# A two-layer encoder trunk on one core: an earlier pool for the FFN up stage, one addition for v, and down tiles that alternate

## The chip, the cores and the metric

The kernel runs on one core of one Trainium2 chip. The metric is the device time of one execution in microseconds (us). Three runs of a kernel give its median.

## What is computed

512 positions of 1024 features go through two layers in float32. Each layer is a token mixer and a gated convolutional FFN, both behind an RMS norm and added to x. Layer 0's mixer joins four trailing-mean pools with a short gated convolution; layer 1's is gated linear attention. The FFN, which the change is mostly about:

```python
def conv_ffn(h, w_up, conv_w, conv_b, w_down):
    u, v = jnp.split(h @ w_up, 2, axis=-1)          # 1024 -> 2 x 2816
    u = causal_dwconv(u, conv_w, conv_b)            # 3 taps along the positions
    return (jax.nn.gelu(u, approximate=False) * v) @ w_down

def reference(x, ...):
    for l in range(DEPTH):                          # 2
        hn = rmsnorm(x, mix_norm[l])
        if l % 2 == 0: y = concat(pool_mixer(...), sb * causal_dwconv(sc * sx, ...)) @ ab_w_out
        else:          y = gla_mixer(hn @ gla_w_in, ...) @ gla_w_out
        x = x + y
        x = x + conv_ffn(rmsnorm(x, ffn_norm[l]), ...)
    return rmsnorm(x, final_norm)
```

## The kernel before

**Data and precision.** Features lie on the 128 partitions, the 512 positions along the free dimension. A float32 factor is split in two parts, hi (rounded by ScalarE, ACT) and lo (the rest, by VectorE, DVE), and a product is three passes of TensorE (PE) matmuls: hi·hi, hi·lo, lo·hi. `split` (L154) does this, with ACT at L155 and DVE at L156.

**Order.** One program is written out; the Tile framework keeps each engine's instructions about in the order of the calls and sets semaphores where a tile is written, read or its buffer reused. Each engine (PE, DVE, ACT, GpSimd or POOL, and SP, which issues the loads) then works through its own list in order. An instruction that waits holds up all behind it on its engine.

**Stages, in the profile's time.** Projections for layer 0's mixers (0 to 100 us), their output projection `abo` (to 144), the up stage of layer 0 (to 380), the down stage (to 500), attention (to 671), its output projection `go` (to 715), the up stage of layer 1 (to 947), the down stage and the final norm. `norm_rows` sums squares with PE, computes the reciprocal root on DVE (L267 to L275, the reciprocal at L271), forms `diag` (L285) and has PE broadcast it (`bc`, L296), which ACT copies to `rs`. `mix_out` also calls `mix_tokens`, which forms the sums and differences of x that the up stage needs (`th`, `tl`).

**Up stage.** 22 tiles of 128 columns for u and for v. The first and last are plain: 48 matmuls of 128x512. The other 20 ("S") use `seven`: the 2x2 block product (rows of w by halves, positions by halves) with seven half-size products p1 to p7 in place of eight, each of 12 matmuls of 128x256. Their weights are:

- a1, the raw left half (SP's load L447, 512 KB, one buffer serves the left halves in turn), split; read by p1 (first half) and p2 (second half)
- s31, a sum of two quarters: SP loads one quarter twice (L439), a GpSimd load adds two more to it (L443, an accumulating DMA); three buffers in the pool "up"; split for p5 and p7
- s2 = −s31 − left (DVE L469), in the free part of the right half's buffer; split into `sh`, `sl` for p6
- a2, the raw right half (SP's load L451, 256 KB) beside left − s2 (DVE L471), split; for p4 and p3

The split parts of a1, s31 and a2 go round four buffers (pool `wsp`). The products accumulate in three PSUM banks: x (p1, p6, p7, p4, with copies k1, k2, k3 taken by ACT in between), y (p2), z (p5, p3). Then

```python
u[hi_t] = -z - k3            # L533, after p7
u[lo_t] = -x                 # ACT, after p4;  u *= rs  L539
v[lo_t] = y + k1             # L520, after p2
v[hi_t] = z + k2             # L544, after p3
```

and u goes through the convolution (ACT L348, DVE L349 and L352) and Gelu (ACT L403); L545 multiplies with v. The steps of all tiles are sorted by hand-given times: tile j starts at `base`, PERIOD later than the one before, the products stand at base + LAYOUT[p], the loads and splits at the offsets in the code.

**Pools.** "side" (y_h of layer 0's mixers, attention's `vtok`, the last four m tiles) and "up" (s31, sh, sl) are opened in turn in one stretch of memory: `open_stage` closes the one and opens the other, so that the first tiles of "up" wait for the last reader of "side". At the start "side" is open; `ffn_up` opens "up", and "side" opens again at the last up tile.

**Down stage.** Eight output tiles; each takes 22 m tiles in blocks of 8, 7 and 7 with one load a block. `split_m` makes the hi and lo parts of m during the last plain tile.

## Time and profile before

| | |
|---|---|
| median of 3 runs | 1082.75 us (1082.29, 1082.75, 1085.55) |
| profiled execution, own time | 1081.99 us |
| its span, first to last instruction | 1080.3 us |
| mean granted TensorE clock | 0.989 |
| PE busy | 1047.6 us, 97% |
| DVE busy | 741.1 us, 69% |
| ACT busy | 543.4 us, 50% |
| GpSimd busy | 52.7 us, 5% |
| HBM read | 132.77 MB, 125 GB/s over the span |
| left and plain up loads of 512 KB, issue to landing | 4.0 us (median of 48) |
| s31 loads; accumulating loads | 4.7 us; 7.4 us (medians of 40) |

Durations in the profile are of one instruction. A row of the timeline gives start, duration, engine, line and operation, `out<-in` by the program's names, and in brackets the idle time of the engine before it with what ended it. Matmuls overlap, so their spacing, not their duration, is what counts. A row of the stretches gives the length, then the busy time of each engine with its count of instructions. In the profile the s31 tiles are called `s`, the copies `k`, the banks `stx`, `sty`, `stz`.

### The profile page before, as it was taken

The page shows a single profiled execution, that of the slowest core. Times are in us where ns is not written, and L with a number is a line of the kernel's source. Part 1 is how long each engine was busy: PE and PEld are TensorE (multiplying, and loading weights), DVE is VectorE, ACT ScalarE, POOL GpSimd, SP SyncE. Part 2 cuts the span into 40 slices and gives each one's busy share as a digit, 9 for nine tenths or more (in the row PEclk, how much of TensorE's full clock was granted, in tenths as well). Part 3 has the DMA queues.
Part 4 walks back from the last instruction along what each step waited for, and adds up shares of the span by engine and source line. Part 5 has one row for each costly group of instructions (what it writes and reads, how often), then busy time and mean ns, then how long its engine had stood idle before and what let it go on. Part 6 is the DMA issues. An engine that isn't in the chain of part 4 may idle for free.

```text
span 1080.3 us, 16455 instructions
## 1 busy us (share of the span) xinstructions
PE 1047.6 (97%) x6586; PEld 937.4 (87%) x6586; DVE 741.1 (69%) x1116; ACT 543.4 (50%) x825; POOL 52.7 (5%) x79
## 2 busy tenths in 40 slices
PE   9999978999999999999999999999999999999996
PEld 7788868999999988889988888879999999988886
DVE  6885758889888874335465565687888888873333
ACT  6342646656656662224773354565556656662221
POOL 0000010110110000000000001001010110000000
PEclk9999998999999999999999999999999999999998
DMA  6421276777765433323332117236777775433312
GB/s 221 144 78 59 79 178 171 186 190 174 186 167 136 130 90 108 97 86 106 94 104 93 42 43 172 63 114 155 168 183 177 184 180 128 130 89 109 96 47 78
DMA packets 53645, 135.94 MB, mean 126 GB/s; under 512 B 4704, under 2 KB 7136, under 8 KB 53568
## 3 DMA queue, kind: packets, MB, share of 16 engines
q1 hardware_dynamic: 41456, 112.74, 34.6%
q0 software_dynamic: 10880, 20.97, 11.9%
q10 hardware_dynamic: 1232, 1.17, 0.3%
q8 instruction: 51, 0.84, 0.3%
q14 instruction: 26, 0.21, 0.1%
HBM read 132.77 MB, written 2.10 MB: 125 GB/s over the span
## 4 chain that ended last, share of the span: by engine, by line
PE 65%; DVE 16%; DMA 11%; issue 6%; ACT 2%; DVEq 0%; SPq 0%; ACTq 0%
PE dn L239 22%; DMA raw<-in_w_up 9%; PE stx L502 7%; PE r L239 4%; PE abo L239 4%; PE go L239 4%; DVE lo L156 3%; PE q L239 2%; PE k L239 2%; PE px L239 2%; PE pb L239 2%; PE stz L502 2%; DVE raw L469 2%; DVE cacc L352 2%; DVE cacc L545 2%
## 5 line engine op out<-in xcount | busy, mean ns | idle before, releaser
L156 DVE TENSOR_TENSOR lo<-raw,hi 128x1024 fp32r<-128x1024 f32 (+2 forms) x191 | 227.7, 1192 | 90.8 <-PE dn L239 50.5
L155 ACT ACTIVATE hi<-raw 128x1024 fp32r<-128x1024 f32 (+2 forms) x191 | 197.3, 1034 | 182.4 <-PE dn L239 101.4
L348 ACT ACTIVATE cacc<-u,colt 128x512 f32<-128x512 f32 x48 | 39.2, 816 | 101.5 <-DVE u L539 91.8
L239 PE MATMUL dn<-mh,hi 128*128 128x512 f32 (+1 forms) x374 | 89.2, 377 | 0.0
L239 PE MATMUL dn<-mh,lo 128*128 128x512 f32 (+1 forms) x374 | 88.7, 377 | 0.0
L239 PE MATMUL dn<-ml,hi 128*128 128x512 f32 (+1 forms) x374 | 88.6, 376 | 0.0
L443 POOL DMA_DIRECT2D s<-in_w_up x40 | 48.2, 1205 | 696.1 <-DVE lo L156 219.3
L239 PEld LDWEIGHTS dn<-mh,hi 128*128 128x128 f32 x374 | 67.5, 188 | 13.4 <-ACT mh L155 0.5
L239 PEld LDWEIGHTS dn<-ml,hi 128*128 128x128 f32 x374 | 67.5, 188 | 12.9
L239 PEld LDWEIGHTS dn<-mh,lo 128*128 128x128 f32 x374 | 67.5, 188 | 12.8
L502 PE MATMUL stx<-th,hi 128*128 128x256 f32 x320 | 55.0, 294 | 8.0 <-ACT k L511 7.1
L349 DVE SCALAR_TENSOR_TENSOR cacc<-u,colt,cacc 128x511 f32<-128x511 f32 x48 | 36.0, 751 | 35.4 <-ACT cacc L348 35.4
L502 PEld LDWEIGHTS stx<-th,hi 128*128 128x128 f32 x320 | 42.8, 188 | 16.0 <-ACT k L511 15.1
L254 ACT ACTIVATE xh<-xall,colt 128x512 fp32r<-128x512 f32 x32 | 22.9, 721 | 59.7 <-DVE xall L334 58.8
L502 PE MATMUL stx<-tl,hi 128*128 128x256 f32 x320 | 49.7, 278 | 0.0
L502 PE MATMUL stx<-th,lo 128*128 128x256 f32 x320 | 49.7, 278 | 0.0
L156 DVE TENSOR_TENSOR lo<-s,hi 128x1024 fp32r<-128x1024 f32 x40 | 48.7, 1217 | 0.6 <-ACT hi L155 0.6
L155 ACT ACTIVATE hi<-s 128x1024 fp32r<-128x1024 f32 x40 | 41.9, 1048 | 9.9 <-DMA s<-in_w_up 9.3
L469 DVE SCALAR_TENSOR_TENSOR raw<-s,raw 128x512 f32<-128x512 f32 x40 | 27.6, 691 | 27.5 <-DMA raw<-in_w_up 17.8
L502 PEld LDWEIGHTS stx<-tl,hi 128*128 128x128 f32 x320 | 42.7, 188 | 0.0
L502 PEld LDWEIGHTS stx<-th,lo 128*128 128x128 f32 x320 | 42.6, 188 | 0.0
L511 ACT ACTIVATE k<-stx 128x256 f32<-128x256 f32 x120 | 40.6, 366 | 2.5 <-PE stx L502 2.4
(289 smaller groups left out, 2305.0 us busy)
## 6 DMA issues: line engine op xcount, KB each, us to landing
raw<-in_w_up SPq DMA_DIRECT2D x48, 512.0 KB, 4.0
s<-in_w_up SPq DMA_DIRECT2D x40, 512.0 KB, 4.7
s<-in_w_up POOLq DMA_DIRECT2D x40, 512.0 KB, 7.4
raw<-in_w_dn SPq DMA_DIRECT2D x32, 448.0 KB, 3.3
raw<-in_w_up SPq DMA_DIRECT2D x40, 256.0 KB, 4.2
raw<-in_w_dn SPq DMA_DIRECT2D x16, 512.0 KB, 3.5
raw<-in_w_qkr SPq DMA_DIRECT2D x16, 512.0 KB, 3.6
raw<-in_w_ab SPq DMA_DIRECT2D x14, 512.0 KB, 3.5
```

The lines of the kernel that those rows point to most:

```text
L155: S.activation(hi, src, AF.Copy)
L156: V.tensor_tensor(lo, src, f32(hi), ALU.subtract)
L239: PE.matmul(out, w[:, k, :], a[k], start=first and i == 0 and k == 0, stop=last and i == 2 and k == n - 1)
L254: S.activation(xh[k], x[k], AF.Copy, scale=col(gname, k))
L348: S.activation(acc, u, AF.Identity, bias=col(bname, j), scale=col(wname, 2 * nj + j))
L349: V.scalar_tensor_tensor(acc[:, 1:], u[:, : T - 1], col(wname, nj + j), acc[:, 1:], ALU.mult, ALU.add)
L352: V.scalar_tensor_tensor(acc[:, 2:], u[:, : T - 2], col(wname, j), acc[:, 2:], ALU.mult, ALU.add)
L443: G.dma_start(w["s31"].rearrange("p (a n) -> p a n", a=2), src, accum_op=ALU.add)
L469: V.scalar_tensor_tensor(s2, s31[:, QUARTER:], -1.0, r[:, :QUARTER], ALU.mult, ALU.subtract)
L502: PE.matmul(b[out][:, :H], wt[:, ks[k]], a[k], start=first and i == 0 and k == 0, stop=i == 2 and k == HK - 1, skip_group_check=True,)
L511: S.activation(q[name], b["x"][:, :H], AF.Copy)
L545: V.tensor_tensor(q["a"], q["v"], q["a"], ALU.mult)
```

## The change

1. The pool "up" is open from the start of the kernel, and y_h of layer 0 takes general slots instead of "side". In layer 1 it is opened ahead of `mix_out("go")`. The s31 loads of the first three S tiles of layer 0 need nothing else and move up in SP's order, to between the first projection blocks; so do their accumulating loads on GpSimd.
2. p2 goes from the second place in a tile to behind p4. p2 and p5/p3 share one bank ("yz", halves by columns), k1 and k2 are written into one tile of 512 columns, and one addition of 128x512 gives v. u's first line (−z − k3) now reads the bank that p2 writes next. The right half's load, a2's split and p4 get slightly other times. A tile has two banks instead of three, and the pool of half tiles two buffers instead of five.
3. The first two down tiles alternate by blocks (tile 0 block 0, tile 1 block 0, tile 0 block 1, ...), and the splits of m are spread over the last plain tile and the first blocks of the down stage.

```diff
--- before.py
+++ after.py
@@ -40,9 +40,10 @@
 QUARTER = HK * P
 UP_KINDS = "PSSSSSSSSSSSSSSSSSSSSP"
 TILE_ORDER = (0, 4, 1, 5, 2, 6, 3, 7)
-LAYOUT = {"p1": 0, "p2": 1, "p6": 3, "p5": 5, "p7": 6, "p4": 9, "p3": 11}
+LAYOUT = {"p1": 0, "p6": 3, "p5": 5, "p7": 6, "p4": 8, "p2": 9, "p3": 11}
 PERIOD = {"S": 7.0, "P": 7.7}
 DOWN_K = (8, 7, 7)
+DOWN_AT = (0, 8, 15)
 
 COLS = {}
 _n = 0
@@ -66,7 +67,7 @@
     big = ctx.enter_context(tc.tile_pool(name="big", bufs=NBIG))
     wp = ctx.enter_context(tc.tile_pool(name="wp", bufs=3))
     wsp = ctx.enter_context(tc.tile_pool(name="wsp", bufs=4))
-    hp = ctx.enter_context(tc.tile_pool(name="hp", bufs=5))
+    hp = ctx.enter_context(tc.tile_pool(name="hp", bufs=2))
     sp = ctx.enter_context(tc.tile_pool(name="sp", bufs=2))
     ps = ctx.enter_context(tc.tile_pool(name="ps", bufs=8, space=bass.MemoryType.PSUM))
 
@@ -84,7 +85,7 @@
     def side(dt=F32, name="s"):
         return stage["side"].tile([P, T], dt, tag="s", name=name)
 
-    open_stage("side")
+    open_stage("up")
 
     def half(name):
         return hp.tile([P, H], F32, tag="h", name=name)
@@ -168,11 +169,8 @@
                 if UP_KINDS[j] == "P":
                     yield w_up[l, j, :, :D], KD, P
                     yield w_up[l, j, :, D:], KD, P
-            for j in range(KD):
-                k0 = 0
-                for kt in DOWN_K:
-                    yield w_dn[l, j, :, k0 * P : (k0 + kt) * P], kt, P, SKEW * (l == 1 and j == KD - 1)
-                    k0 += kt
+            for j, k0, kt in down_blocks():
+                yield w_dn[l, j, :, k0 * P : (k0 + kt) * P], kt, P, SKEW * (l == 1 and j == KD - 1)
             if l == 0:
                 off = 0
                 for n, ks in zip(VG_COLS, VG_K):
@@ -393,7 +391,6 @@
         }
         ms = [None] * NF
         events = []
-        open_stage("up")
 
         def at(t, fn):
             events.append((t, len(events), fn))
@@ -479,19 +476,19 @@
             at(base - 17, load_sum)
             at(base - 12.5, add_sum)
             at(base - 10, load_left)
-            at(base - 4.5, load_right)
+            at(base - 4.2, load_right)
             at(base - 6, prep_a)
             at(base - 4, prep_b)
             at(base - 1, prep_c)
-            at(base + 3, prep_d)
+            at(base + 2, prep_d)
 
             left = {
                 "p1": ("a1", 0), "p2": ("a1", 1), "p6": ("s2", 0), "p5": ("s31", 1), "p7": ("s31", 0),
                 "p4": ("a2", 1), "p3": ("a2", 0),
             }
 
-            def product(name, out, first):
-                if first:
+            def product(name, out, first, ts=lo_t):
+                if out not in b:
                     b[out] = bank("st" + out)
                 piece, side = left[name]
                 ks = [slice(side * QUARTER + k * P, side * QUARTER + (k + 1) * P) for k in range(HK)]
@@ -500,37 +497,33 @@
                 for i, (wt, a) in enumerate(((h, ah), (h, al), (lo, ah))):
                     for k in range(HK):
                         PE.matmul(
-                            b[out][:, :H], wt[:, ks[k]], a[k],
+                            b[out][:, ts], wt[:, ks[k]], a[k],
                             start=first and i == 0 and k == 0, stop=i == 2 and k == HK - 1,
                             skip_group_check=True,
                         )
                 tick()
 
-            def keep(name):
-                q[name] = half(name)
-                S.activation(q[name], b["x"][:, :H], AF.Copy)
+            def keep(dst):
+                S.activation(dst, b["x"][:, :H], AF.Copy)
 
             def run_p1():
                 product("p1", "x", True)
-                keep("k1")
-
-            def run_p2():
-                product("p2", "y", True)
-                q["v"] = slot(name="v")
-                V.tensor_tensor(q["v"][:, lo_t], b["y"][:, :H], q["k1"], ALU.add)
+                q["k"] = slot(name="kk")
+                keep(q["k"][:, lo_t])
 
             def run_p6():
                 product("p6", "x", False)
-                keep("k2")
+                keep(q["k"][:, hi_t])
 
             def run_p5():
-                product("p5", "z", True)
+                product("p5", "yz", True, hi_t)
 
             def run_p7():
                 product("p7", "x", False)
-                keep("k3")
+                q["k3"] = half("k3")
+                keep(q["k3"])
                 q["u"] = slot(name="u")
-                V.scalar_tensor_tensor(q["u"][:, hi_t], b["z"][:, :H], -1.0, q["k3"], ALU.mult, ALU.subtract)
+                V.scalar_tensor_tensor(q["u"][:, hi_t], b["yz"][:, hi_t], -1.0, q["k3"], ALU.mult, ALU.subtract)
 
             def run_p4():
                 product("p4", "x", False)
@@ -539,10 +532,13 @@
                 V.tensor_tensor(u, u, rs, ALU.mult)
                 q["a"] = gate(j, u)
 
+            def run_p2():
+                product("p2", "yz", False, lo_t)
+
             def run_p3():
-                product("p3", "z", False)
-                V.tensor_tensor(q["v"][:, hi_t], b["z"][:, :H], q["k2"], ALU.add)
-                V.tensor_tensor(q["a"], q["v"], q["a"], ALU.mult)
+                product("p3", "yz", False, hi_t)
+                V.tensor_tensor(q["k"], b["yz"], q["k"], ALU.add)
+                V.tensor_tensor(q["a"], q["k"], q["a"], ALU.mult)
 
             for name, fn in (("p1", run_p1), ("p2", run_p2), ("p6", run_p6), ("p5", run_p5), ("p7", run_p7),
                              ("p4", run_p4), ("p3", run_p3)):
@@ -566,44 +562,50 @@
                 if j > last_s and not closed:
                     closed = True
                     at(base + 5.2, lambda: open_stage("side"))
-                if j > last_s + 1 or j == NF - 1:
-                    for i in range(5):
-                        at(base + (i + 0.5) * PERIOD["P"] / 5, lambda: split_m(2))
+                    for i in range(4):
+                        at(base + 5.3 + 0.6 * i, lambda: split_m(2))
             else:
                 seven(j, base)
             base += PERIOD[kind]
         at(base - 3.0, lambda: ensure(item + 1))
         for _, _, fn in sorted(events, key=lambda e: e[:2]):
             fn()
-        split_m(NF)
-        return mh, ml
-
-    def ffn_down(l, mh, ml, finish, halves_last=False):
-        for j in range(KD):
-            blocks, k0 = [], 0
-            split_now = halves_last and j == KD - 1
-            o = None if split_now else bank("dn")
-            for i, kt in enumerate(DOWN_K):
-                h, lo = weights()
-                if split_now:
-                    blocks.append((h, lo, k0, kt))
-                else:
-                    accumulate(o, h, lo, mh[k0 : k0 + kt], ml[k0 : k0 + kt], i == 0, i == len(DOWN_K) - 1)
-                k0 += kt
-            if not split_now:
-                finish(j, o)
+        return mh, ml, split_m
+
+    def down_blocks():
+        for k0, kt in zip(DOWN_AT, DOWN_K):
+            for j in range(2):
+                yield j, k0, kt
+        for j in range(2, KD):
+            for k0, kt in zip(DOWN_AT, DOWN_K):
+                yield j, k0, kt
+
+    def ffn_down(l, mh, ml, split_m, finish, halves_last=False):
+        o = {}
+        late = []
+        for j, k0, kt in down_blocks():
+            split_m(k0 + kt + 3 * j - len(mh))
+            h, lo = weights()
+            if halves_last and j == KD - 1:
+                late.append((h, lo, k0, kt))
+                continue
+            if j not in o:
+                o[j] = bank("dn")
+            last = k0 + kt == NF
+            accumulate(o[j], h, lo, mh[k0 : k0 + kt], ml[k0 : k0 + kt], k0 == 0, last)
+            if last:
+                finish(j, o[j])
                 tick()
-                continue
-            for half in range(2):
-                ts = slice(half * 256, half * 256 + 256)
-                o = bank("dn")
-                for i, (h, lo, k0, kt) in enumerate(blocks):
-                    accumulate(
-                        o[:, :256], h, lo,
-                        [m[:, ts] for m in mh[k0 : k0 + kt]], [m[:, ts] for m in ml[k0 : k0 + kt]],
-                        i == 0, i == len(DOWN_K) - 1, step=tick,
-                    )
-                finish(j, o, half)
+        for half in range(2 if late else 0):
+            ts = slice(half * 256, half * 256 + 256)
+            b = bank("dn")
+            for h, lo, k0, kt in late:
+                accumulate(
+                    b[:, :256], h, lo,
+                    [m[:, ts] for m in mh[k0 : k0 + kt]], [m[:, ts] for m in ml[k0 : k0 + kt]],
+                    k0 == 0, k0 + kt == NF, step=tick,
+                )
+            finish(KD - 1, b, half)
 
     acc = slot(name="acc")
 
@@ -630,7 +632,7 @@
     for k in range(KD):
         square_acc(k, acc)
 
-    y_h = [side(F32R, "yh") for _ in range(8)]
+    y_h = [slot(F32R, "yh") for _ in range(8)]
     y_l = [slot(F32R, "yl") for _ in range(8)]
     _, rs = norm_rows(acc, 1, 2)
 
@@ -686,14 +688,14 @@
     mixed = mix_out("abo", "ffn0", acc)
 
     _, rs = norm_rows(acc, 1, 2)
-    mh, ml = ffn_up(0, rs, mixed)
+    down = ffn_up(0, rs, mixed)
     acc = slot(name="acc")
 
     def down_out(j, o):
         V.tensor_tensor(o, o, rs, ALU.mult)
         residual(j, o, "mix1", acc)
 
-    ffn_down(0, mh, ml, down_out)
+    ffn_down(0, *down, down_out)
 
     starts = slot(name="starts")
     G.memset(starts, 1.0)
@@ -925,11 +927,12 @@
         gate_r(i)
 
     acc = slot(name="acc")
+    open_stage("up")
     mixed = mix_out("go", "ffn1", acc)
     assert not pending
 
     _, rs = norm_rows(acc, 1, 2)
-    mh, ml = ffn_up(1, rs, mixed)
+    down = ffn_up(1, rs, mixed)
     acc = slot(name="acc")
 
     def last(j, o, half=None):
@@ -977,7 +980,7 @@
         else:
             after(2, one)
 
-    ffn_down(1, mh, ml, last, True)
+    ffn_down(1, *down, last, True)
 
 
 _OUTS = [((D, T), "float32")]
```

## The prediction

> **What bounds the kernel now.** I read the page first: the engines' shares, the chain, and the row with the largest wait for a transfer.
>
> ```profile
> span 1080.3 us, 16455 instructions
> PE 1047.6 (97%) x6586; PEld 937.4 (87%) x6586; DVE 741.1 (69%) x1116; ACT 543.4 (50%) x825; POOL 52.7 (5%) x79
> ...
> PE 65%; DVE 16%; DMA 11%; issue 6%; ACT 2%; DVEq 0%; SPq 0%; ACTq 0%
> ...
> L469 DVE SCALAR_TENSOR_TENSOR raw<-s,raw 128x512 f32<-128x512 f32 x40 | 27.6, 691 | 27.5 <-DMA raw<-in_w_up 17.8
> ```
>
> TensorE (PE) is busy 97% of the span, so in all about 33 us of its idle time can be won, beside whatever a busy PE loses to slowed matmuls. VectorE (DVE) is busy 69% and yet has 16% of the chain; DMA has 11%. The last row says where they meet: L469, the first DVE instruction to read a tile's left half, sat idle 17.8 of 27.5 us for its load.
>
> Then the stretches. I chose the bounds at the start of each up stage and at the change to the down stage.
>
> ```profile
> core 0: us, PE busy (x) PEld busy (x) DVE busy (x) ACT busy (x) POOL busy (x), PEclk, DMA share, GB/s
> ...
> 144.00:167.00 23.00, 13.19 (x60) 10.40 (x60) 13.01 (x25) 7.87 (x11) 3.74 (x3) 0.84 0.87 199
> 167.00:380.00 213.00, 209.54 (x1730) 204.05 (x1729) 185.67 (x271) 132.72 (x215) 20.40 (x17) 0.99 0.68 167
> 380.00:500.00 120.00, 120.00 (x530) 99.16 (x529) 55.07 (x70) 39.98 (x54) 2.83 (x13) 1.00 0.32 98
> ...
> 732.00:947.00 215.00, 210.47 (x1725) 204.22 (x1725) 183.43 (x267) 130.91 (x213) 19.26 (x16) 1.00 0.67 162
> ```
>
> The columns that matter are the second and third (length, PE busy). The start of the first up stage (144 to 167) has 9.81 us of PE idle at a clock of 0.84. The body of the first up stage has 3.5, that of the second 4.5. The first down stage has none. So there are two places to look at: the opening of the first up stage, and the pace of its tiles.
>
> **The opening of the first up stage.** Next the timeline there, queue by queue, and the same place in the second layer.
>
> ```profile
> 144.48 0.89 SPq L439 DMA_DIRECT2D s<-in_w_up  x2
> ...
> 149.96 1.33 POOL L443 DMA_DIRECT2D s<-in_w_up  x1 [147.64 <-DVE tb L371]
> ...
> 151.66 0.17 DVE L271 RECIPROCAL y<-s 128x4 f32<-128x4 f32 x1
> 160.65 0.69 DVE L469 SCALAR_TENSOR_TENSOR raw<-s,raw 128x512 f32<-128x512 f32 x1 [8.82 <-DMA s<-in_w_up]
> ...
> 166.36 0.80 PE L296 MATMUL bc<-diag,ones_r 128*128 128x512 f32 x1 [9.81 <-DVE diag L285]
> ...
> 730.10 0.80 PE L296 MATMUL bc<-diag,ones_r 128*128 128x512 f32 x1 [2.90 <-DVE diag L285]
> ```
>
> The s31 load (`s<-in_w_up`) is issued at 144.48, GpSimd's accumulating load at 149.96, and DVE sits 8.82 us until 160.65 for it. Behind that L469 in DVE's order stand the last steps of the norm and the two `diag` products, for which PE waits 9.81 us at 166.36. In layer 1, where the "up" pool's s31 loads had gone out long before, the same wait is 2.90.
>
> The change opens the pool at the start of the kernel, and the built order shows the three s31 loads at SP's 17th, 18th and 21st places, among the first projection blocks; GpSimd's accumulates wait for them alone. They will have been there for 100 us when DVE reaches L469. What is late next is DVE's own work between the reciprocal at 151.66 and `diag`, the same instructions as in layer 1. So I take the wait of layer 1 for what is left: 9.81 − 2.90, **−6.9 us**. The ends: 8.8, all of DVE's idle time, and 6, if DVE takes one more split of 0.7 ahead of `diag` than layer 1 does. Layer 1 opens the pool a little earlier in the text, but its loads keep their places in SP's order: 0. y_h of layer 0 moves from the side pool to the general slots; no instruction of the first 144 us gets a new wait in the built order, so 0.
>
> **What the early loads cost at the start.** Now three loads of 512 KB and three accumulates stand among the w_ab loads that PE waits for.
>
> ```profile
> 27.06 1.22 DVE L156 TENSOR_TENSOR lo<-raw,hi 128x1024 fp32r<-128x1024 f32 x1 [1.69 <-ACT hi L155]
> ...
> 31.68 1.06 ACT L155 ACTIVATE hi<-raw 128x1024 fp32r<-128x1024 f32 x1 [2.48 <-DMA raw<-in_w_ab]
> ...
> 30.63 0.39 PE L296 MATMUL bc<-diag,ones_r 128*128 128x512 f32 x1
> ...
> 37.83 0.50 PE L657 MATMUL po<-ph,pwh 128*128 128x512 f32 x1 [1.11 <-ACT ph L155]
> ...
> DMA to landing us min/median/max: 3.3/3.4/5.3
> ...
> DMA to landing us min/median/max: 6.4/6.4/6.4
> ...
> DMA to landing us min/median/max: 8.8/8.8/8.8
> ```
>
> The path there: `lo` at 27.06 has waited 1.69 us for its load and ACT's `hi`, and the steps of the norm up to `diag` stand behind it in DVE's order, so that PE's `bc` comes at 30.63; its buffer then takes the load that ACT waits for until 31.68; and the mixer's `ph` reaches PE at 37.83, which has idled 1.11. From there PE is dense, so what is lost here is carried whole. The three answers on landing are the four w_ab loads issued from 18.8 to 28.3; one load of w_go issued at 647 among three s31 loads, with their accumulates behind; and the left load issued at 150 beside the three accumulates. The nearest price is the second: 6.4 against the first's median of 3.4, +3.0. The far one is the third, 8.8, +5.4. The two loads on the path follow each other, so that each can lose something, but 3 MB more at the 199 GB/s of the stretch from 144 are over in 16 us, and the first two s31 loads go out ahead of the loads that are on the path. I take **+3.5**, near the closer row; ends 0 (if they slip into the gaps between w_ab's loads) and +5.4.
>
> The Trainium skill ("DMA: Bandwidth & Descriptors", section "Queues, rings and completion order") says that each DMA engine takes turns between the queues that have work. By that a load beside one busy software queue at most doubles, 3.4 to 6.8, which would make this term +3.4; the 647 row agrees, the 8.8 is beyond it.
>
> **The pace of the up tiles.** Twenty tiles in each layer run as seven products. I took one whole tile from DVE's timeline, with SP's load of the left half and two passes of PE.
>
> ```profile
> 842.41 1.22 DVE L156 TENSOR_TENSOR lo<-s,hi 128x1024 fp32r<-128x1024 f32 x1
> ...
> 845.88 0.42 DVE L533 SCALAR_TENSOR_TENSOR u<-stz,k 128x256 f32<-128x256 f32 x1
> 846.22 0.69 DVE L471 TENSOR_TENSOR raw<-raw 128x512 f32<-128x512 f32 x1
> 846.82 0.42 DVE L520 TENSOR_TENSOR v<-sty,k 128x256 f32<-128x256 f32 x1
> ...
> 848.28 0.69 DVE L539 TENSOR_TENSOR u<-u,rs 128x512 f32<-128x512 f32 x1
> 849.86 0.75 DVE L349 SCALAR_TENSOR_TENSOR cacc<-u,colt,cacc 128x511 f32<-128x511 f32 x1 [0.89 <-ACT cacc L348]
> 851.39 0.69 DVE L469 SCALAR_TENSOR_TENSOR raw<-s,raw 128x512 f32<-128x512 f32 x1 [0.78 <-DMA raw<-in_w_up]
> ...
> 852.99 1.22 DVE L156 TENSOR_TENSOR lo<-s,hi 128x1024 fp32r<-128x1024 f32 x1
> ...
> 846.97 0.33 SPq L447 DMA_DIRECT2D raw<-in_w_up  x1
> ...
> 846.29 0.62 PE L502 MATMUL stx<-tl,sh 128*128 128x256 f32 x4
> 846.74 0.62 PE L502 MATMUL stx<-th,sl 128*128 128x256 f32 x4
> ...
> DMA to landing us min/median/max: 3.5/3.8/5.4
> ...
> DMA to landing us min/median/max: 3.6/4.1/4.7
> ```
>
> A pass of four matmuls is 0.45 us (846.29 to 846.74); 21 passes are 9.5, the floor of a tile of seven products. This tile took 10.58 (842.41 to 852.99). It is a loop through the one buffer for left halves: L469 is its first reader, L471 (846.22) its last; then SP loads (846.97), and L469 at 851.39 waits for that. From L469 to L471 DVE works 1.60 + 3.81 = 5.41; L471 and the issue add 0.75; the load 4.42. So the period is about 6.16 + load, or 9.9 to 10.3 with the medians of 3.8 and 4.1 and 0.1 for the hand-over. DVE's own sum is a second limit: 9.8 with the 0.89 of idle before L349, in which it waits for ACT's L348. The stages show these periods, from p2 to p2:
>
> ```profile
> 176.84 0.62 PE L502 MATMUL sty<-xh,hi 128*128 128x256 f32 x4
> 205.40 0.61 PE L502 MATMUL sty<-xh,hi 128*128 128x256 f32 x4
> 358.08 0.62 PE L502 MATMUL sty<-xh,hi 128*128 128x256 f32 x4
> 741.04 0.63 PE L502 MATMUL sty<-xh,hi 128*128 128x256 f32 x4
> 925.44 0.62 PE L502 MATMUL sty<-xh,hi 128*128 128x256 f32 x4
> ```
>
> (358.08 − 205.40)/15 is 10.18, (925.44 − 741.04)/18 is 10.24. The three tiles before them, (205.40 − 176.84)/3, take 9.52, PE's floor, so no gain is to be had from them.
>
> After the change p2 (second half of a1) runs late in a tile, behind p4. The last reader of the left half becomes `lo` of a1, which waits for ACT's `hi`, which takes the buffer that p2 reads until its second pass is over; p2 in turn waits for L533's u, because it now shares u's bank. The loop from L469 in the new order: L469, `lo` of s31 and u, 2.33 less 0.16 of overlap (845.88 to 846.22 shows 0.34 for 0.42) = 2.17; two passes of p2, 0.91; `hi` of a1, 1.06; `lo`, 1.22; the hand-offs between engines some 0.55 (an estimate: the rows show 0.07 from L471's end to SP's issue, and DVE to PE or PE to ACT some 0.2). That is **5.9 + load**, against 6.26 with the same hand-over. DVE's sum has no 0.89 any more, since `lo` of a1 stands in that place in the built order; one addition of 0.69 takes the place of two of 0.42 that overlapped, which is nothing. So DVE needs about 8.9 to 9.3, below PE's floor.
>
> The load is the same load in the same company (s31's is issued 3 to 4 us ahead of it in both), so I leave it at 3.8 and 4.1. The gain is 6.26 − 5.92 = 0.34 a tile over 15 + 18 tiles: **−11.2 us**. The ends: PE's floor in every tile, 15 x 0.66 + 18 x 0.72 = −22.9; and 0, if the load grows by what the loop loses.
>
> p2's new wait is the one added to PE's order. Behind it stand the other products; u comes some 2.4 us after p7's end (`hi` of s31, 1.06, starts when p7's second pass is over and is done 0.8 after p7; `lo` 1.22, u 0.42), p2's turn 2.7 (two products of three passes). So 0.3 is left, and a late load goes straight through to PE; that is in the loop above.
>
> The Trainium skill ("PSUM — Partial Sum Buffer", section "PSUM bank collisions raise a hardware error") has it that two engines must not touch one bank at once even at different columns, so that this wait cannot be dropped although p2 and u use different halves. No run here shows a collision.
>
> **Down stages.** Alternating the first two tiles by blocks gives the last m tiles more time to be split. The stretch from 380 is 120.00 of 120.00 busy: there is no wait to remove. Cover if it goes wrong: the splits are now made as needed, on engines busy 46% and 33% there. 0, ends ±0.5.
>
> **Sum.** −6.9 + 3.5 − 11.2 = −14.6. The profiled execution's own time is 1081.99, so 1067.4; the median of the three runs, 1082.75, stands 0.8 higher: **1068**.
>
> **Rivals.** *The loads eat the pace.* The tiles run faster, so the same bytes fall closer (DMA is busy 0.68 in the body of the stage), and the left load grows by 0.3. For it: L469 already waits 17.8 us for them. Against: 4% more load on queues a third idle. Then 1082.75 + 3.5 − 6.9 = 1079.4, about no change. Chance 0.14.
>
> *PE at its floor.* If `lo` of a1 comes earlier than the loop says, loads up to 4 us hide: 1082.75 − 3.4 − 22.9 = 1056.5. For it: the three tiles at 9.52. Chance 0.10.
>
> *The start costs more.* Both loads on the path at 8.8 us, +10.8: with the other terms 1075.5. Against: 3 MB are not enough. Chance 0.08.
>
> *Slower: the tight ring.* The new loop passes through PE twice and ACT once, each in order. If each of the four crossings costs 0.2 to 0.3 more than I gave, because the instruction in front is late (`hi` of s31 ahead of k3, u·rs ahead of `lo` of a1), the loop is 6.8 + load, 10.75 a tile: 33 x 0.54 = +17.8, together 1082.75 + 3.5 − 6.9 + 17.8 = 1097. It decides from a loop constant of 6.36, or a period of 10.31. For it: four buffers for hi and lo in both orders, and p2 holds one longer. Chance 0.13.
>
> The forecast itself has 0.55. About 0.3%, 3.2 us, is what a measurement of this kernel can tell from no change. Faster by more: the forecast, the floor, the start and half of the first rival, 0.80. Same: the other half, 0.07. Slower: 0.13. The range leaves out the slower rival and part of the floor: 1057 to 1081; the forecast's own is 1062 to 1074.
>
> **What would show it.** PE's wait before the first `bc` of layer 0's up stage near 3, not 9.8. The mixer's first `po` at 40 to 43 where it was 37.83. p2 to p2 at 9.7 to 10.0 in the steady tiles, DVE with no wait before L349's counterpart but a short one at `lo` of a1 for PE, and L469's wait below 17.8. Wrong is the forecast if the tiles stay at 10.2 or PE waits at the first pass of p2 in most tiles, or if the w_ab loads near 20 us land later than 10 us after issue.

## The result and the profile after

The changed kernel takes 1071.39 us (median of 4 runs, 1067.80 to 1073.32), the kernel before 1082.88 (4 runs). The ratio is 0.9885, 95% interval 0.9853 to 0.9917: 1.2% faster. The forecast was 1068, its range 1057 to 1081. The profiled execution took 1070.47, its span is 1068.8.

First the page of the changed kernel: span, engines, and the chain by engine and by line.

```profile
span 1068.8 us, 16387 instructions
PE 1044.1 (98%) x6586; PEld 939.1 (88%) x6586; DVE 745.2 (70%) x1076; ACT 554.0 (52%) x825; POOL 52.7 (5%) x79
...
PE 86%; DVE 5%; DMA 5%; ACT 2%; issue 2%; DVEq 0%; SPq 0%; ACTq 0%
PE dn L237 22%; PE stx L499 17%; PE styz L499 14%; PE r L237 4%; PE abo L237 4%; PE go L237 4%; DMA raw<-in_w_up 3%; DVE lo L157 3%; PE q L237 2%; PE k L237 2%; PE px L237 2%; PE pb L237 2%; DMA raw<-in_w_ab 2%; PE pc L237 2%; PE vg L793 1%
```

The chain has moved to PE: 86% where it was 65%, DVE 5% for 16%, DMA 5% for 11%. The waits for up-stage loads are 3% of it, formerly 9%. Next the stretches that answer to those of before (their bounds follow the stages, which now begin earlier).

```profile
core 0: us, PE busy (x) PEld busy (x) DVE busy (x) ACT busy (x) POOL busy (x), PEclk, DMA share, GB/s
144.00:164.00 20.00, 17.86 (x81) 14.39 (x80) 17.74 (x32) 11.17 (x17) 0.49 (x1) 0.96 0.47 141
164.00:370.00 206.00, 202.21 (x1701) 199.61 (x1700) 181.46 (x242) 134.52 (x209) 19.91 (x17) 1.00 0.67 166
370.00:490.00 120.00, 120.00 (x536) 99.59 (x536) 58.81 (x76) 41.79 (x57) 2.83 (x13) 1.00 0.34 102
731.00:937.00 206.00, 204.36 (x1698) 201.38 (x1698) 183.31 (x244) 134.83 (x211) 19.26 (x16) 1.00 0.66 166
```

The opening (144 to 164) has 2.1 us of PE idle instead of 9.8; the up stages keep 3.8 and 1.6 us of idle. From the PE timelines of both kernels I read where each stage begins, and took the differences:

| from the PE timeline, us | before | after | change of this part |
|---|---|---|---|
| mixer's first `po` | 37.83 | 41.73 | +3.9 |
| first `bc` of up stage 0 | 166.36 | 162.61 | −7.7 beyond that |
| from there to the first `dn` of layer 0 | 213.66 | 212.29 | −1.4 |
| to the first `bc` of up stage 1 | 350.08 | 349.76 | −0.3 |
| from there to the first `dn` of layer 1 | 217.29 | 211.95 | −5.3 |
| to the end of the span | 132.90 | 132.16 | −0.7 |

The sum is −11.5. Three places carry it: a loss at the start, the gain at the first opening, and a gain in the second up stage; the first up stage gained little.

The waits of PE at these places, from the timelines after, with two rows of ACT among them; ahead of them stand two loads from the chain of work that leads to `po` (start, time to landing):

```profile
24.95 7.94 DMA raw<-in_w_ab
...
35.34 4.66 DMA raw<-in_w_ab
...
40.10 1.06 ACT L156 ACTIVATE hi<-raw 128x1024 fp32r<-128x1024 f32 x1 [1.92 <-DMA raw<-in_w_ab]
...
32.55 0.60 PE L294 MATMUL bc<-diag,ones_r 128*128 128x512 f32 x1 [2.23 <-DVE diag L283]
41.73 0.50 PE L659 MATMUL po<-ph,pwh 128*128 128x512 f32 x1 [1.20 <-ACT ph L156]
...
162.61 0.79 PE L294 MATMUL bc<-diag,ones_r 128*128 128x512 f32 x1 [2.14 <-DVE diag L283]
171.85 0.74 PE L499 MATMUL stx<-th,hi 128*128 128x256 f32 x4 [1.51 <-ACT kk L507]
174.19 0.62 PE L499 MATMUL styz<-th,hi 128*128 128x256 f32 x3 [0.69 <-ACT hi L156]
...
169.60 1.28 ACT L400 ACT_TABLE_LOAD   x1
...
724.66 0.49 PE L294 MATMUL bc<-diag,ones_r 128*128 128x512 f32 x1 [2.76 <-DVE diag L283]
```

The wait for `diag` is 2.14 and the one of layer 1 is still 2.76, as was to be expected of it. At the start the wait of 2.23 is new (`bc` had none at 30.63); the one of 1.20 at `po` was there before, with 1.11. What makes `po` late is the loads: the w_ab load issued at 24.95 took 7.94 us, where the one issued at 24.73 before took 3.31, and ACT waits until 40.10 for the one issued at 35.34, with `ph` behind it in its order. New is the pair at 171.85 and 174.19: ACT's table load for Gelu, 1.28 us at 169.60, stands ahead of `kk`, and p7 waits 1.51 for that; the split of s31 behind it makes p5 wait 0.69.

Now the pace. The rows are passes of four matmuls, first around 204.7, then one tile later on, from its p2 to the next, then the first pass of p6 at the ends of the steady tiles of both stages.

```profile
204.29 0.62 PE L499 MATMUL stx<-th,lo 128*128 128x256 f32 x4
204.74 0.68 PE L499 MATMUL styz<-xh,hi 128*128 128x256 f32 x4
205.26 0.63 PE L499 MATMUL styz<-xl,hi 128*128 128x256 f32 x4
...
825.01 0.64 PE L499 MATMUL styz<-xh,hi 128*128 128x256 f32 x4
825.48 0.64 PE L499 MATMUL styz<-xl,hi 128*128 128x256 f32 x4
...
834.90 0.63 PE L499 MATMUL styz<-xh,hi 128*128 128x256 f32 x4
...
206.20 0.63 PE L499 MATMUL stx<-th,sh 128*128 128x256 f32 x4
354.23 0.62 PE L499 MATMUL stx<-th,sh 128*128 128x256 f32 x4
737.60 0.62 PE L499 MATMUL stx<-th,sh 128*128 128x256 f32 x4
915.73 0.64 PE L499 MATMUL stx<-th,sh 128*128 128x256 f32 x4
```

834.90 − 825.01 is a tile of 9.89 us. PE does not wait in it, and yet it is not at the 9.52 that I had called its floor: a pass takes 0.47 us (825.01 to 825.48), where it took 0.45 up to 204.74 (204.29 to 204.74). That is 117.7 ns from one matmul to the next instead of 113.3. The slow rhythm begins at 204.74, the first pass of a p2, after a hardly visible wait (its weight load starts some 50 ns late), and stays for the next eight tiles. The granted clock is 1.00 in both.

The last four rows give the mean. p2 has moved, so I count from p6 to p6: 15 tiles take 148.03 us (354.23 − 206.20), 9.87 each, and 18 take 178.14 (915.73 − 737.60), 9.90 each. Before, the same tiles took 152.68 and 184.30, or 10.18 and 10.24 each. So the steady tiles gained 4.7 and 6.2 us, and the stages of the table only 1.4 and 5.3. The rest, 3.3 and 0.8 us, was lost in front of and behind these tiles, nearly all of the 3.3 in front; the waits of p7 and p5 shown above are 2.2 of it.

The loads that were the bound before are shown by their landing (left halves, both up stages after) and by the idle time of their first reader on DVE in the stretch 745 to 910, after and before:

```profile
DMA to landing us min/median/max: 3.5/3.6/4.6
...
DMA to landing us min/median/max: 3.5/3.7/4.5
...
  DMA raw<-in_w_up: 2.9, 6
...
  DMA raw<-in_w_up: 10.9, 13
```

The left halves land in 3.6 and 3.7 us, and DVE waits 2.9 us for them where it waited 10.9.

### The profile page after: what moved, and what is told of

The parts are those of the page before. It is cut to its first block, busy times and chain, and to the rows that moved or that the text cites. A ratio compares the mean times of both kernels' runs of the same rounds, so it can differ in the third digit from the quotient of the medians.

```text
span 1068.8 us, 16387 instructions
## 1 busy us (share of the span) xinstructions
PE 1044.1 (98%) x6586; PEld 939.1 (88%) x6586; DVE 745.2 (70%) x1076; ACT 554.0 (52%) x825; POOL 52.7 (5%) x79
## 4 chain that ended last, share of the span: by engine, by line
PE 86%; DVE 5%; DMA 5%; ACT 2%; issue 2%; DVEq 0%; SPq 0%; ACTq 0%
PE dn L237 22%; PE stx L499 17%; PE styz L499 14%; PE r L237 4%; PE abo L237 4%; PE go L237 4%; DMA raw<-in_w_up 3%; DVE lo L157 3%; PE q L237 2%; PE k L237 2%; PE px L237 2%; PE pb L237 2%; DMA raw<-in_w_ab 2%; PE pc L237 2%; PE vg L793 1%
## 5 line engine op out<-in xcount | busy, mean ns | idle before, releaser
L499 PE MATMUL styz<-xh,hi 128*128 128x256 f32 x320 | 51.2, 282 | 3.0 <-DVE u L526 3.0
L499 PE MATMUL stx<-th,hi 128*128 128x256 f32 x320 | 50.2, 279 | 1.5 <-ACT kk L507 1.5
L499 PE MATMUL styz<-xl,hi 128*128 128x256 f32 x320 | 50.1, 279 | 0.0
L499 PE MATMUL styz<-xh,lo 128*128 128x256 f32 x320 | 50.1, 279 | 0.0
L499 PEld LDWEIGHTS styz<-xh,hi 128*128 128x128 f32 x320 | 43.1, 188 | 4.9 <-DVE u L526 4.6
L499 PEld LDWEIGHTS styz<-xl,hi 128*128 128x128 f32 x320 | 43.0, 189 | 0.0
```

What stands on the lines that cost most here:

```text
L499: PE.matmul(b[out][:, ts], wt[:, ks[k]], a[k], start=first and i == 0 and k == 0, stop=i == 2 and k == HK - 1, skip_group_check=True,)
```

## The experiments

Each was timed in five rounds beside the kernel before on the same chip. The chips differ: the kernel before has a median of 1088.25 with the first four, 1084.98 with the next four, 1089.74 with the last three. So ratios are compared, not times. The edits are shown abridged.

**Part 1 alone.** The kernel before with the pool open from the start and y_h in general slots.

```diff
-    open_stage("side")          # at the kernel's start
+    open_stage("up")
-    y_h = [side(F32R, "yh") for _ in range(8)]
+    y_h = [slot(F32R, "yh") for _ in range(8)]
-        open_stage("up")        # in ffn_up; now ahead of mix_out("go")
```

> The kernel before with part 1 alone (the pool "up" open from the start, y_h of layer 0 in general slots). My theory: the start loses 3.9 us (the mixer's first po near 41.7 instead of 37.83), PE's wait before the first bc of layer 0's up stage falls from 9.8 to 2-3, and the tiles keep their pace of 10.2: 7.7 - 3.9 = 3.8 us less than before, some 1079. Rival: the earlier s31 loads also set the pace of the tiles, then part 1 gives most of the 11.5 us, some 1072.

Measured: ratio 0.9993 (0.9979 to 1.0008), no change that can be told. Both terms are there, in PE's timeline:

```profile
42.53 0.50 PE L656 MATMUL po<-ph,pwh 128*128 128x512 f32 x1 [1.17 <-ACT ph L155]
...
163.46 0.80 PE L296 MATMUL bc<-diag,ones_r 128*128 128x512 f32 x1 [2.21 <-DVE diag L285]
```

`po` comes at 42.53 and the wait at `bc` is 2.21. But the up stage that follows takes 219.66 us, and 217.40 in the next experiment but one, which has the old opening on the same chip: there three tiles after the first run at 9.52 us, here two. A likely reason is that the long wait had let loads get ahead and the tiles lived on that for a while; no run tests it by itself. Against that profile (`po` at 37.73, a wait of 8.11 at `bc`) the start lost 4.8 us, the opening gained 5.9, and 2.3 were given back in the stage: no gain is left. The rival falls, and my −3.8 was too much.

**Part 2 alone.** Order of the products, shared bank, one addition for v; times of load, split and p4 as in the change.

```diff
-LAYOUT = {"p1": 0, "p2": 1, "p6": 3, "p5": 5, "p7": 6, "p4": 9, "p3": 11}
+LAYOUT = {"p1": 0, "p6": 3, "p5": 5, "p7": 6, "p4": 8, "p2": 9, "p3": 11}
...
-    product("p2", "y", True)
+    product("p2", "yz", False, lo_t)
```

> The kernel before with part 2 alone (p2 late, one bank for p2, p5 and p3, one addition for v). My theory: start and opening as before (po at 37.8, PE's wait 9.8), the tiles at 9.5 to 9.9 instead of 10.2, so 6.7 to 9 us less than before, 1074 to 1076. Rival: the pace comes from the other parts, then no change, or a loss by p2's new wait.

Measured: 0.9858 (0.9833 to 0.9883), more than I expected and no less than the whole change (0.9885, on another chip). The up stages take 212.42 and 212.03 us, where those of part 3 alone, with the old order on this chip, take 217.40 and 223.67. Part 2 carries the gain. The landing of the left halves in the second up stage shows a part that I had left out; the rows are part 1 alone, part 3 alone and part 2 alone, on one chip:

```profile
DMA to landing us min/median/max: 3.6/4.3/5.1
...
DMA to landing us min/median/max: 3.5/4.5/5.2
...
DMA to landing us min/median/max: 3.5/3.8/5.4
```

With the old loop the load takes 4.3 and 4.5 us, with the new one 3.8. The same loads land sooner in the new order.

**Part 3 alone.** The first two down tiles by blocks in turn, the splits spread.

```diff
-            for j in range(KD):
-                k0 = 0
-                for kt in DOWN_K:
+            for j, k0, kt in down_blocks():
...
+        split_m(k0 + kt + 3 * j - len(mh))
```

> The kernel before with part 3 alone (the first two down tiles by blocks in turn, the splits of m spread). My theory: PE has no wait at the start of a down stage, so nothing, within 0.5 us of before. Rival: the last splits of m do hold PE up there in small waits, then 1 to 2 us less.

Measured: 0.9992 (0.9972 to 1.0012). Nothing, as expected.

**The pool opened later.** The changed kernel; "side" is open first and holds one tile of the second convolution group, so "up" can only begin when that has been read.

```diff
-    open_stage("up")            # at the kernel's start
+    open_stage("side")
-        c = scaled(pc, rs, "u")
+        c = scaled(pc, rs, "u", side if j == 1 else slot)
+    open_stage("up")            # ahead of mix_out("abo")
```

> The changed kernel with one edit: the pool "up" opens only when a tile of the second convolution group (c of j = 1, held in "side") has been read, so that the first three s31 loads and their accumulates go out near 90 us and not among the first w_ab loads. My theory: the start is that of before (po at 37.8), the opening of the up stage stays at a wait of 2 to 3, so 3.9 us less than the changed kernel, some 1067.5. Rival: the same 3 MB delay the w_abo loads there instead and PE waits for these, so that the gain is below 1 us.

Measured: 0.9815 (0.9788 to 0.9842). Against the changed kernel's 0.9885 and 0.9884, both from other chips, this is 0.7% or 7 us, where 3.9 was expected; the intervals are wide enough for that. The places are as expected:

```profile
38.22 0.50 PE L660 MATMUL po<-ph,pwh 128*128 128x512 f32 x1 [1.20 <-ACT ph L157]
...
159.09 0.50 PE L295 MATMUL bc<-diag,ones_r 128*128 128x512 f32 x1 [2.18 <-DVE diag L284]
```

`po` at 38.22, and the wait at `bc` stays at 2.18. The loss at the start belonged to the place of the s31 loads and their accumulating loads.

**The changed kernel again,** for the next three.

> The changed kernel again, beside the runs of before on the same chip as the next three, so that they can be compared with it. Expected: 11 to 19 us less than before, since where the loads of the left halves land later (4.2 to 4.5 us in the experiments so far, 3.8 to 4.1 in the first profile) before loses and the changed kernel does not.

Measured: 0.9884 (0.9858 to 0.9910).

**A bank of its own for p2.** Then p2 needn't wait for u, and v takes two additions again.

```diff
-    product("p2", "yz", False, lo_t)
+    product("p2", "y", True, lo_t)
-    V.tensor_tensor(q["k"], b["yz"], q["k"], ALU.add)
+    for ts, name in ((lo_t, "y"), (hi_t, "yz")):
+        V.tensor_tensor(q["k"][:, ts], b[name][:, ts], q["k"][:, ts], ALU.add)
```

> The changed kernel with a bank of its own for p2 again, and so two additions of 128x256 for v: p2 no longer waits for u. If p2's wait costs its own idle time and also throws PE into the slower rhythm (117.8 ns from matmul to matmul instead of 113.3, seen to begin at the first matmul of p2), both up stages come to 9.5 us a tile throughout: 5 us of waits and 8 us of rhythm, up to 10 us less than the changed kernel. Rival: the wait moves to another product (p3 for u, p4 for k3) and the rhythm sets in there; then less than 3 us.

Measured: 0.9812 (0.9773 to 0.9850), 7 us below the changed kernel. In the profile the up stages take 204.60 and 204.55 us. Two stretches of this kernel, then of the changed one on the same chip; the column to read is PE busy with its count of matmuls:

```profile
core 0: us, PE busy (x) PEld busy (x) DVE busy (x) ACT busy (x) POOL busy (x), PEclk, DMA share, GB/s
205.00:350.00 145.00, 145.00 (x1282) 145.00 (x1281) 136.42 (x199) 98.19 (x152) 15.62 (x13) 1.00 0.71 182
745.00:910.00 165.00, 165.00 (x1452) 164.78 (x1451) 154.66 (x223) 112.18 (x174) 18.06 (x15) 1.00 0.70 179
...
205.00:350.00 145.00, 144.77 (x1224) 143.97 (x1223) 130.86 (x175) 93.93 (x145) 15.62 (x13) 1.00 0.70 174
745.00:910.00 165.00, 163.45 (x1423) 162.64 (x1422) 152.48 (x204) 109.17 (x170) 18.05 (x15) 1.00 0.73 181
```

With its own bank PE is busy 145.00 of 145.00 and does 1282 matmuls there, 113.1 ns each. The changed kernel is busy 144.77 and does 1224, 118.3 ns each. So in these stretches the sharing cost 1.8 us of waits and, in this execution, more by the rhythm that follows a wait. The rival is not seen: no other product waits. The runs of this kernel spread from 1057.37 to 1068.76, and the profile is of one of the two shortest (1057.77; the other four took 1064.88 or more), so its 11 us below the changed kernel's profile are more than the 7 of the medians.

**A second buffer for left halves, changed kernel.** The odd tiles' left halves get a buffer of their own.

```diff
-NBIG = 41
+NBIG = 40
+    lp = ctx.enter_context(tc.tile_pool(name="lp", bufs=1))
-    w["raw", 0] = wp.tile([P, WBLK], F32, tag="raw", name="raw")
+    w["raw", 0] = (wp, lp)[j % 2].tile([P, WBLK], F32, tag="raw", name="raw")
```

> The changed kernel with a second buffer for the left halves (own buffer for the odd tiles, one general slot less): a load is out of the loop, its reader finds it there. If the loop through the left buffer still sets u's lateness, L466's wait (some 5 us) and p2's (3 to 5 us) go: 4 to 6 us less, more if the slow rhythm goes with them. Rival: PE's floor and rhythm set the pace already: within 2 us.

Measured: 0.9832 (0.9805 to 0.9860), some 5.6 us below the changed kernel. The up stages take 209.02 and 209.21 against 214.17 and 208.82. The start loses 2.2 more (`po` at 43.81), since the new buffer is free at the start too and a fourth load goes out there.

**The same second buffer, kernel before.** This tells the loop through the one buffer from DVE's own sum.

> The kernel before with a second buffer for the left halves (own buffer for the odd tiles, two general slots less), nothing else. My theory of the loop (period = 6.2 + load through the one buffer): L469's wait goes and the tiles fall to DVE's own sum, 9.8 us: 0.35 us or more a tile over 33 tiles, 10 to 15 us less than before. Rival: DVE's sum with its 0.89 us of idle before L349 is the bound by itself: no change.

Measured: 0.9829 (0.9791 to 0.9867), a gain of 1.7% by one buffer, without a part of the change: some 18 us where 10 to 15 were expected. From the second up stage: who waited for the left loads (nobody) and their landing, the group of the first convolution step on DVE, and the stretch.

```profile
who waited for it (us, times):
busy tenths in 40 slices 0000000000000000000000000000000000000000
DMA to landing us min/median/max: 3.6/4.8/6.7
...
L350 DVE SCALAR_TENSOR_TENSOR cacc<-u,colt,cacc 128x511 f32<-128x511 f32 x17 | 12.7, 748 | 3.2 <-ACT cacc L349 3.2
...
745.00:910.00 165.00, 164.75 (x1454) 164.56 (x1453) 154.38 (x222) 107.71 (x171) 18.06 (x15) 1.00 0.73 177
```

The load takes 4.8 us now, longer than ever, and nobody waits for it. PE is busy 164.75 of 165.00 with 1454 matmuls, 113.3 ns each: PE's floor. DVE idles 3.2 us in 17 tiles for ACT's L349 (L348 of before), 0.19 a tile, where I had counted 0.89 as part of DVE's sum. The loop was the bound; DVE's sum was none.

**Later pool and own bank together.**

> The changed kernel with the pool opened later (as in e4_later) and a bank of its own for p2 (as in e5_own). If the two losses are independent, the start is that of before (po near 38) and the up stages run at 9.5 us a tile: 11 us less than the changed kernel from the bank in the profile of e5_own and 4 from the start, a profile's span near 1052, some 2.5 to 3% below before. Rival: with the start back the loads fall otherwise and the waits and the slow rhythm come back: a span of 1060 or more.

Measured: 0.9722 (0.9702 to 0.9742), within what was expected. The profile has a span of 1058.6, not 1052, and shows why, in the same two stretches:

```profile
205.00:350.00 145.00, 145.00 (x1234) 145.00 (x1233) 132.28 (x189) 93.68 (x146) 15.62 (x13) 1.00 0.71 174
745.00:910.00 165.00, 165.00 (x1452) 164.74 (x1451) 153.81 (x222) 109.39 (x172) 18.07 (x15) 1.00 0.71 179
```

PE is busy in all of both. In the first stage it does 1234 matmuls in 145 us (117.5 ns each), in the second 1452 in 165 (113.6). The first stage fell into the slow rhythm at its beginning, and as no product had to wait any more, nothing took it out: 211.43 us for 204.60.

**And the second left buffer with it.**

> e9_later_own with a second buffer for the left halves as well (own buffer for the odd tiles, one general slot less). If PE is the bound of every tile in e9_later_own, this adds nothing to the span (within 2 us) but makes the runs agree better, as a late load then reaches nobody. Rival: waits that e9_later_own still has go, 2 to 5 us less.

Measured: 0.9735 (0.9703 to 0.9768). Nothing added, as expected; but the runs do not agree better, they go from 1051.86 to 1064.62. That was wrong.

**Second left buffer and later pool in the kernel before,** without parts 2 and 3.

> The kernel before with the second buffer for the left halves and the pool opened late (part 1 with the late opening), without parts 2 and 3. If the loop through one left buffer is what part 2 really relieved, this does as well as the changed kernel with its start mended: the tiles at 9.5 to 9.9 and the opening's wait at 2 to 3 us, 1056 to 1062. Rival: the changed order of the products has a gain of its own; then it stays 5 us or more above e9_later_own in both up stages together.

Measured: 0.9672 (0.9648 to 0.9696), 1054.26 us: the fastest of all, 35 us below the kernel before on this chip. The kernel of the experiment before this one has the same two edits and the new order with its own bank (and part 3, which gave nothing alone); its ratio of 0.9735 lies clearly above 0.9672. So beside a second buffer the new order has no gain of its own here, rather a loss. The profiles can't size it: the up stages take 205.48 and 209.39 here, 207.05 and 203.69 there, but that execution is the shortest of its six (1051.86) and this one the longest of its own (1057.59). The first opening, where 2 to 3 us were expected, has no wait left:

```profile
156.23 1.98 PE L420 MATMUL u<-xh,lo 128*128 128x512 f32 x8
158.05 0.40 PE L298 MATMUL bc<-diag,ones_r 128*128 128x512 f32 x1
```

## Why the prediction was right, point by point

**The start: +3.5 forecast, +3.9 found.** The place and the path were right: w_ab loads land late, `bc` and `po` come late with them, and the rest carries it. The size was in part luck. The w_ab loads issued from 18.4 to 25.0 took 4.1, 8.2 and 7.9 us to land, the latter two near the far row (8.8) and not the close one (6.4). The last of them is on the chain and lost 4.6, against the 3.0 of the row that I leaned on; slack that I had not counted took up the difference. Those two landings are also beyond the doubling that I had drawn from the Trainium skill ("DMA: Bandwidth & Descriptors", section "Queues, rings and completion order"), by which 3.4 becomes at most 6.8; two accumulating loads and an s31 load of SP's own queue were in flight beside each, more than the one busy queue that I had reckoned with. The later pool shows that it is the place of the loads of s31.

**The opening: −6.9 forecast, −7.7 found.** Right as it was told: DVE's own work up to `diag` is what came late next. Not foreseen was what follows: Gelu's table load in front of p7 (1.51 us) and the split in front of p5 (0.69). Part 1 alone (short wait, old order) has none at p7, part 2 alone (long wait, new order) 0.36 us, and p2's own bank (short wait, new order) 0.05, so what brings it on stays open. I had written that the first three tiles run at PE's floor and have nothing to gain. They could lose: in part 1 alone one of them did. In the changed kernel they kept 9.6, and the loss lay in front of them.

**The pace: −11.2 forecast, −10.8 found in the steady tiles that it was reckoned for (4.7 and 6.2), −6.7 over the whole stages.** The sum put nothing at the first tiles of the stages, where 3.3 us of the difference went in layer 0. The mechanism was right. That the loop through one left buffer set the period, at about 6.2 plus the load, is shown by the second buffer in the kernel before. (With the 0.1 for the hand-over its range was 10.1 to 10.4 and not 9.9 to 10.3; the step from 6.26 to 5.92 has it on both sides.) That −10.8 comes so close to −11.2 is luck, for three terms of the sum were off:

- The load. I kept it at 3.8 and 4.1; it fell to 3.6 and 3.7, and on another chip from 4.3 and 4.5 to 3.8. With 5.9 + 3.65 the new loop is at PE's floor of 9.5, so more should have come out, not less.
- The floor. I took 9.52 for it. In the first up stage as many matmuls as make 8 tiles and in the second as make 13 ran in the slow rhythm, in which a tile takes 9.89. That is the term that was mis-sized: 0.37 us a tile.
- DVE's second limit, 9.8. It is none; the idle 0.89 was slack that shrinks when nothing else is late.

That the forecast of 9.7 to 10.0 a tile came true is thus owed to two errors that cancel.

**p2's wait.** The 0.3 us of margin were about right: p2 waited in 8 of the 40 tiles, up to 0.77 us, and for 3.0 us in all by the page. What I had not seen is what such a wait does to the tiles after it.

**Down stages: 0.** Right, by part 3 alone. The parts of the table that hold the down stages changed by −0.3 and −0.7, but part 2 alone, without part 3, shows the same (349.79 and 132.15 us).

**The rivals.** The tight ring did not come: the loop closed within its estimate. The floor is where the mechanism went, without the time that I gave for it. The loads did not get longer with the pace, they got shorter. The start cost 3.9 us and not the 10.8 of the rival, though one load on the path did come near 8.8.

Left open: why the left load lands sooner in the new order, and what decides whether PE takes the slow or the fast rhythm after a wait.

## What to carry to other kernels

Find the loop that a buffer closes (last reader, load, first reader) and add up its period before changing the work inside it; a second buffer for one operand gave here what a new order of seven products gave. A wait that is removed may have been feeding what comes after it, so the removal is to be measured over the following stage too. A load moved to "early" should be given a place, not just the first free one.

## What the runs showed of the hardware

**Two rhythms of the same matmul.** A 128x256 matmul followed the one before by 113.3 ns or by 117.7 ns, for many tiles on end, at a granted clock of 1.00 and with no engine waited for. In the traces of the thirteen profiles, in the steady tiles of the up stages, I counted some 230 places where a matmul came late (over 122 ns behind the one before). Of the 186 that began in the fast rhythm 40 ended in the slow one, of the 43 that began in the slow one 35 ended in the fast; the counts shift by a few with where the steady tiles are taken to begin. Outside such places one change was seen. So a wait of a few hundredths of a us can cost 4% of all that follows, up to the next one, and a kernel that hardly waits can keep either rhythm for a whole stage (the runs with p2's own bank went from 1057.37 to 1068.76). It may well be behind that spread; the profiles are of single executions, and this was not tested by itself.

**The clock after a wait.** In all thirteen traces the granted clock changes only at steps of 3.41 us, counted from its first rise: every stretch of one clock but the last is a whole multiple of that. The first two rows are two such steps of the changed kernel, with the wait of 2.14 us in the first. The last two are steps of the kernel with p2's own bank, where a wait of 2.13 us ended at 33.46. The columns to read are PE busy and, after POOL busy, the granted clock.

```profile
core 0: us, PE busy (x) PEld busy (x) DVE busy (x) ACT busy (x) POOL busy (x), PEclk, DMA share, GB/s
159.09:162.51 3.42, 1.37 (x7) 0.80 (x5) 3.07 (x7) 1.78 (x3) 0.00 (x0) 1.00 0.69 169
162.51:165.92 3.41, 3.31 (x13) 3.12 (x14) 2.51 (x5) 0.60 (x1) 1.19 (x1) 0.50 0.63 173
...
29.71:33.13 3.42, 1.63 (x8) 1.01 (x6) 2.46 (x8) 0.85 (x2) 0.33 (x1) 1.00 0.88 305
33.13:36.54 3.41, 2.98 (x12) 2.24 (x13) 2.33 (x4) 2.38 (x3) 0.87 (x1) 1.00 0.91 205
```

PE was idle for 2.05 us of the first step, and the next ran at half clock. In the other kernel a wait of nearly the same length fell across two steps, 1.79 us of it in the first, and the clock stayed at 1.00. In all thirteen traces up to 1040 us, half clock followed every full-clock step with 1.87 us of idle or more, and none with 1.79 or less. So the length of a wait does not decide alone; its place in the steps does too. The Trainium skill ("TensorE: Matmul & The Clock Gate", section "What's actually happening") puts the drop to half at an idle window of about 3.4 us, one that runs freely. The length of the step agrees; that all of it must be idle does not, and the measurement decides. What a drop costs seems to depend on what else is late; these are comparisons of kernels, not a test. From the first `bc` to p7's first matmul the changed kernel took 9.24 us with a drop, and the kernel with the later pool, without one, 8.28. At the start, from `bc` to `po`, it took 9.18 with a drop, and the kernel with p2's own bank 8.99 without one, as `ph` was late in both.
